# Layer 1 attention: the first bank of the next scores written before the values products, in two iterations

## The chip, the cores and the metric

The kernel runs on one core of a Trainium2 chip. The metric is the device time of one execution in microseconds (us), the median of several runs; less is better.

## The reference, cut to what matters

Two layers work on 512 latent tokens and 256 context tokens of width 1024. Layer 0 mixes by a bidirectional gated DeltaNet, layer 1 by attention with 8 query heads and 2 key heads of width 128. The change is in layer 1's attention alone:

```
def gqa_attend(q, k, v):
    b, lq, hq, d = q.shape
    qg = q.reshape(b, lq, ATT_KV_HEADS, hq // ATT_KV_HEADS, d)
    s = jnp.einsum('bqhgd,bkhd->bhgqk', qg, k).astype(F32) * (d ** -0.5)
    p = jax.nn.softmax(s, axis=-1).astype(v.dtype)
    return jnp.einsum('bhgqk,bkhd->bqhgd', p, v).reshape(b, lq, hq, d)
...
    y_lat = finish(blocked_gqa(ql, k_all, v_all), zl)      # finish: (o * silu(z)) @ w_out
...
return rms_norm(h_lat, final_norm_g)
```

Here `k_all` and `v_all` hold 768 tokens, context and latent ones together; the queries are the 512 latent ones.

## The kernel before

A float32 product is made of three products on TensorE: each operand is kept as a rounded high part and a low part, and `PASS` lists high by high, high by low and low by high.

Attention is one loop written out for `u` in 0 to 35 (`for u in range(32 + 4)`). Each of the first 32 values of `u` stands for one query head `hq = u // 4` and one tile `t = u % 4` of 128 queries. The work is pipelined over iterations. In iteration `u` TensorE issues, in this order:

1. `scores(u)` (line 2260): the 128 x 768 scores of query tile `u`, 6 products into `s3`;
2. `turn(u - 2)` (line 2288): six transposes of the shares of tile `u - 2`;
3. the iteration's extra piece: query or gate projections while there are any (`u` up to 23: lines 2189 and 2240), nothing in iterations 24 and 25, and `out_block(u - 26, 0, pg)` (line 2323), six products of the output projection, in iterations 26 to 32;
4. `values(u2, ...)` (line 2309): half of a pair's products of shares and values, 9 products into `po`. Iterations 24 and 25 make the two halves of pair 10.

Beside it VectorE takes the row maxima of `s3` (`maxima`, lines 2266 and 2268), ScalarE the exponentials with their sums (`powers`, line 2275, which reads the whole half of `s3` of its `u`), VectorE a reciprocal (line 2276), ScalarE the scaled shares (`shares`, line 2281). Transposes are copied out by `turned` (ScalarE, line 2295) and `turned_lo` (VectorE, line 2301). In even iterations `gated` (lines 2315, 2317, 2318) multiplies a finished pair of values by its gate, ahead of the maxima.

`s3` is one tile of PSUM, 128 x 2 x 768 float32, which is three banks of 512. Even `u` use elements 0 to 767 and odd `u` elements 768 to 1535. So each has one bank to itself, called its own bank (elements 0 to 511 or 1024 to 1535), and half of the middle bank, called shared. `scores` makes the three products of 512 columns on the own bank first and then the three of 256 columns on the shared one.

TensorE, VectorE and ScalarE run in the order in which the code is written (`manual_schedule`); the framework puts in the semaphores. GpSimd and the DMA queues are ordered by the framework's planner. GpSimd splits the output weights into `wo` during these iterations (lines 2455 and 2456). In iterations 24 and 25 the maxima are kept in `pg[0]`, in the others in the free half of `po`'s bank. After the loop TensorE makes the rest of the output projection (line 2471), and a short chain of VectorE and ScalarE instructions (lines 2477 to 2557) normalises and sends the last rows.

Of the kernel before, what the change touches and what calls it, by code (L numbers as in the profile page):

```python
# [86 lines left out]
def backbone(tc, a, out):  # L87
# [1137 lines left out]
    for k in range(KT):  # L1225
        for h in steps:
            wh, wl = halves_of[h]
            for i in range(2):
                first = not k
# [58 lines left out]
    c = []  # L1288
# [29 lines left out]
    for n, (i, nb) in enumerate(((0, 4), (0, 5), (1, 0), (1, 2), (1, 1), (1, 3), (1, 4), (1, 5))):  # L1318
# [3 lines left out]
        first, through = nb >= 4 or nb < 2, []  # L1322
# [93 lines left out]
    for pair in range(3):  # L1416
        first = None
# [5 lines left out]
    for t in range(NT):  # L1423
        due = T0 + (185, 80, 315, 190, 30, 335)[t]
        U = [Piece("DVE", 2.15, due, j_turn, t, d, after=[solved[t // 2]] + (joined if t < 5 else []), takes=["U" if t < 5 else "U5"] if d == 0 else (), lands=0.1) for d in range(2)]
        u = U[0].takes[0]
# [764 lines left out]
    def q_squares(p, t):  # L2191
        for h in range(2):
            jk = tmp.tile([P, P], F32, tag="jk", name=f"qj{p}{t}{h}")
            S.activation(jk, q_bank(p, t)[:, h * P:(h + 1) * P], AF.Square, accum_out=qTs["s", p][:, t, h:h + 1])

    def q_cosines(p, t):
        x = q_bank(p, t).rearrange("p (h d) -> p h d", h=2)
        o = tmp.tile([P, 2, P], F32, tag="qr", name=f"qr{p}{t}", bufs=2)
        V.tensor_tensor(o, x, bcast(cg[0][:, t], 1, 2), ALU.mult)
        return o  # L2200

    def q_sines(p, t, o):

        x = q_bank(p, t).rearrange("p (h d) -> p h d", h=2)
        V.tensor_tensor(x, x, bcast(sg[0][:, t], 1, 2), ALU.mult)
        o4 = o.rearrange("p h (s d) -> p h s d", s=2)
        V.tensor_tensor(o4, o4, raw(x, 64, [[128, 2], [-64, 2], [1, 64]]), ALU.add)
# [4 lines left out]
    def q_norm_steps(p, room_, t0, t1):  # L2212

        n = 2 * (t1 - t0)
        s_ = qTs["s", p].rearrange("p t h -> p (t h)")[:, 2 * t0:2 * t1]
        x, t = (room_[:, i * 16:i * 16 + n] for i in range(2))
        y = rsp.tile([P, 8], F32, tag="qy", name=f"qy{p}{t0}")[:, 0:n]
        steps = [
            lambda: V.tensor_scalar(x, s_, 1.0 / P, EPS, ALU.mult, ALU.add),
            lambda: V.tensor_scalar(y.bitcast(I32), x.bitcast(I32), -0.5, float(0x5F3759DF), ALU.mult, ALU.add),  # L2220
        ]
        for i in range(3):
            to = s_ if i == 2 else y
            steps += [
                lambda: V.scalar_tensor_tensor(t, x, -0.5, y, ALU.mult, ALU.mult),
                lambda: V.tensor_tensor(t, t, y, ALU.mult),
                lambda to=to: V.scalar_tensor_tensor(to, t, 1.5, y, ALU.add, ALU.mult),
            ]
        return steps
# [12 lines left out]
    def z_tanh(hq):  # L2242
        zts[hq] = at.tile([P, NLAT], F32, tag="zt", name=f"zt{hq}", bufs=4)
        S.activation(zts[hq], z_bank(hq), AF.Tanh, scale=0.5)
# [5 lines left out]
        z_tanh(hq)  # L2250
        z_rest(hq)

    def scores(u):
        hq, t = divmod(u, 4)
        g, b = hq // 4, u % 2
        own, shared = (slice(0, 512), slice(512, 768)) if b == 0 else (slice(256, 768), slice(0, 256))
        for c in (own, shared):
            for n_, (i, j) in enumerate(PASS):
                q = qTs[hq // 2][i][:, hq % 2, t * P:(t + 1) * P]
                T.matmul(s3[:, b, c], q, kT[j][:, g, c], start=n_ == 0, stop=n_ == 2)  # L2260

    def maxima(u):
        hq, t = divmod(u, 4)
        b = u % 2
        top = (pg[0] if u in (24, 25) else spare)[:, b:b + 1]
        V.tensor_reduce(top, s3[:, b], AX.X, ALU.max, negate=True)
        nm_ = at.tile([P, 1], F32, tag="nm", name=f"nm{u}")
        V.tensor_tensor(nm_, top, qTs["s", hq // 2][:, t, hq % 2:hq % 2 + 1], ALU.mult)
        return nm_
# [13 lines left out]
    def turn(u, ps):  # L2283

        pr, _ = prs.pop(u)
        for i3 in range(2):
            for j in range(3):
                T.transpose(ps[i3][:, j, :], pr[:, (i3 * 3 + j) * P:(i3 * 3 + j + 1) * P], ident)  # L2288

    def turned(u, ps):  # L2290
        t = u % 4
        if t % 2 == 0:
            pTs[u // 2] = [at.tile([P, NT, 256], F32R, tag=f"pT{i}", name=f"pT{u // 2}_{i}") for i in range(2)]
        for i3 in range(2):
            S.copy(pTs[u // 2][0][:, i3 * 3:i3 * 3 + 3, (t % 2) * P:(t % 2 + 1) * P], ps[i3][:, :3])
# [15 lines left out]
    def gated(u2):  # L2311
        hq, c0 = u2 // 2, (u2 % 2) * 256
        pTs.pop(u2)
        y32 = po[:, 0:256]
        V.scalar_tensor_tensor(y32, y32, 0.5, zts[hq][:, c0:c0 + 256], ALU.mult, ALU.mult)
        ys = [y[:, hq, c0:c0 + 256] for y in yT]
        S.copy(ys[0], y32)
        V.tensor_tensor(ys[1], y32, ys[0], ALU.subtract)
# [61 lines left out]
    for u in range(32 + 4):  # L2380
        piece = pieces1[u] if u < len(pieces1) else None
        last = (q_products, 0, 3) if u == 0 else pieces1[u - 1] if u <= len(pieces1) else None
        turning = 2 <= u < 34
        if u < 32:
            scores(u)
        if u >= 6 and u % 2 == 0:
            gated((u - 6) // 2)
        ps = [tr_tile(f"pt{u}_{i3}") for i3 in range(2)]
        o = None
        if last and last[0] is q_products:  # L2390
            q_squares(*last[1:])
            o = q_cosines(*last[1:])
        elif last and u % 2 == 0:
            z_tanh(last[1])
        if u == 0:
            norms = q_norm_steps(0, spare[:, 16:48], 3, 4)
        if turning:
            turn(u - 2, ps)
            turned(u - 2, ps)
        nm_ = maxima(u) if u < 32 else None  # L2400
        if o is not None:
            q_sines(*last[1:], o)
        if turning:
            turned_lo(u - 2, ps)
        if last and last[0] is z_products and u % 2 == 0:
            z_rest(last[1])
        if u < 32:
            powers(u, nm_)
        if u % 8 == 6 and u < 24:
            norms = q_norm_steps(u // 8 + 1, pg[0][:, 256:288], 0, 4)  # L2410
        if u % 8 in (6, 7) or u == 1:
            some(norms, 7 if u % 8 == 6 else 99)
        for half in range(2):
            if piece and piece[0] is q_products:
                q_products(*piece[1:], range(half * 4, half * 4 + 4))
            elif piece:
                k0 = 4 * (u % 2) + 2 * half
                z_products(piece[1], range(k0, k0 + 2))
            elif half == 0 and 26 <= u < 33:
                out_block(u - 26, 0, pg)  # L2420
            elif half == 0 and u >= 33:
                s_all = raw(s3, 0, [[1, 3 * 512]])
                acc1 = [s_all[:, nh * 512:(nh + 1) * 512] for nh in range(2)]
                for k in ((0, 1, 2), (3, 4, 5), ())[u - 33]:
                    out_block(k, 1, acc1)
                if u == 35:
                    out_block(7, 0, pg)
            if half == 1 and o is not None:
                q_turned(*last[1:], o)
            if u == 32 and half == 0:  # L2430
                aq_c.__exit__(None, None, None)
                f2_c = tc.tile_pool(name="fo", bufs=2, side="right", reuse_waits="tile")
                f2 = f2_c.__enter__()
                fg = f2.tile([P, D], F32, tag="fg", name="fg", bufs=1)
                gate1 = f2.tile([P, 1, D], F32, tag="gate1", name="gate1", bufs=1)
                ss = f2.tile([P, 4, 3], F32, tag="ss", name="ss", bufs=1)
                dma(gate1, gate_d[1])
                for t in range(3):
                    load_hs(t)
                dma(fg, a["final_norm_g"].unsqueeze(0).partition_broadcast(P).squeeze(1))  # L2440
                G.tensor_scalar(fg, fg, -(2.0 ** 0.5), None, ALU.mult)
            if half == 1 and u >= 4:
                u2, h_ = divmod(u - 4, 2)
                values(u2, range(3 * h_, 3 * h_ + 3))
        if u < 32:
            shares(u)
        if u == 23:
            gemm_c.__exit__(None, None, None)
            wo_c = tc.tile_pool(name="wo", bufs=2, side="left", reuse_waits="tile")
            wp = wo_c.__enter__()  # L2450
            wo = [wp.tile([P, KT, D], F32R, tag=f"wo{i}", name=f"wo{i}", bufs=1) for i in range(2)]
            for k in range(KT):
                w = wp.tile([P, D], F32, tag="w", name=f"wf{k}", bufs=3)
                dma(w, a["att_w_out"][0, k * P:(k + 1) * P, :])
                G.tensor_copy(wo[0][:, k], w)
                G.tensor_tensor(wo[1][:, k], w, wo[0][:, k], ALU.subtract)
# [146 lines left out]
```

## Time and profile before

| | us |
|---|---|
| median of 3 runs | 1144.64 |
| lowest and highest run | 1141.11, 1145.9 |
| the profiled execution, device time | 1139.69 |
| the profiled execution, span from first to last instruction | 1137.5 |
| TensorE busy | 1106.4 (97% of the span) |
| VectorE, ScalarE, GpSimd busy | 787.5, 746.9, 603.1 |

A line of the timeline gives the start of a run of like instructions, the time from its start to its end, engine, line, what is written from what, and the count; the bracket gives the idle time of the engine ahead of it and what ended it. PE is TensorE's products, PEld its weight loads, DVE VectorE, ACT ScalarE, POOL GpSimd. Products overlap in TensorE's pipeline, so that a run's end lies some 0.25 us behind the start of the next.

### The profile page before, as it was taken

To read this page: it belongs to the slowest core of one execution; us is meant where nothing else is said; L and a number is where in the kernel's file an instruction comes from. 1 tells how busy PE (TensorE), PEld (TensorE's weight loads), DVE (VectorE), ACT (ScalarE), POOL (GpSimd) and SP (SyncE) were. 2 spreads that over 40 slices of the span, in tenths; PEclk is the share of its full clock that TensorE was granted. 3 is DMA by queue.
4 is the path that set the end of the run, shared out by engine and by line. 5 is a ranking of instruction groups with operands and counts; after the bars stand their busy time and mean duration, and the time that the engine had idled before them with its cause. 6 is when DMAs were issued, how large, how long until landed. Compare 5 with 4: busy or idle time off the path is not lost. (4 is left out here: it accounts for less than half of the span.)

```text
span 1137.5 us, 27228 instructions
## 1 busy us (share of the span) xinstructions
PE 1106.4 (97%) x10511; PEld 903.7 (79%) x10511; DVE 787.5 (69%) x1628; ACT 746.9 (66%) x1990; POOL 603.1 (53%) x525
## 2 busy tenths in 40 slices
PE   5999999999999999999999999999999999999997
PEld 2677788888888888888666666788877889989886
DVE  4785666688889988774678788445555477667647
ACT  4453554477787888756689888875776356666731
POOL 0564111329999999960675598656744353130820
PEclk9999999999999999999999999999999999999999
DMA  9489753765738887665998994676854112101323
GB/s 366 180 305 324 253 159 118 228 174 171 219 129 245 280 233 222 182 229 164 280 279 249 276 257 116 207 213 183 247 148 139 37 58 73 38 19 57 111 75 93
DMA packets 117106, 208.69 MB, mean 183 GB/s; under 512 B 12113, under 2 KB 76786, under 8 KB 111730
## 3 DMA queue, kind: packets, MB, share of 16 engines
q1 hardware_dynamic: 97202, 195.71, 55.8%
q10 hardware_dynamic: 19776, 11.25, 3.3%
q8 instruction: 83, 1.36, 0.5%
q14 instruction: 45, 0.37, 0.1%
HBM read 166.16 MB, written 40.67 MB: 182 GB/s over the span
## 5 line engine op out<-in xcount | busy, mean ns | idle before, releaser
L1768 PE MATMUL po<-woh,y 128*128 128x512 f32 x384 | 129.3, 401 | 0.0
L1706 POOL TENSOR_TENSOR wol<-wo,woh 128x1024 fp32r<-128x1024 f32 x32 | 77.3, 2416 | 54.3 <-ACT woh L1699 51.1
L810 POOL TENSOR_TENSOR X<-X,tmp 128x62 f32<-128x62 f32 (+15 forms) x93 | 99.5, 1070 | 7.3
L1594 POOL TENSOR_TENSOR S<-S,glb 128x512 f32<-128x512 f32 x80 | 81.8, 1044 | 36.4 <-PE ks L1585 36.1
L809 POOL TENSOR_TENSOR tmp<-L,X 128x62 f32<-128x62 f32 (+15 forms) x93 | 91.0, 979 | 6.7
L929 PE MATMUL g_z<-uh,wh_z 128*128 128x512 f32 (+1 forms) x256 | 88.0, 344 | 0.0
L929 PE MATMUL g_v<-uh,wh_v 128*128 128x512 f32 (+1 forms) x256 | 87.9, 344 | 0.0
L944 DVE SCALAR_TENSOR_TENSOR acc_v<-g_v,cwv,acc_v 128x510 f32<-128x510 f32 (+3 forms) x128 | 77.7, 614 | 14.7 <-ACT acc_v L936 11.3
L929 PE MATMUL g_z<-ul,wh_z 128*128 128x512 f32 (+1 forms) x256 | 86.2, 337 | 0.5 <-issue 0.5
L929 PE MATMUL g_v<-ul,wh_v 128*128 128x512 f32 (+1 forms) x256 | 86.1, 336 | 0.0
L929 PE MATMUL g_v<-uh,wl_v 128*128 128x512 f32 (+1 forms) x256 | 86.1, 336 | 0.0
L929 PE MATMUL g_z<-uh,wl_z 128*128 128x512 f32 (+1 forms) x256 | 86.1, 336 | 0.0
L1768 PEld LDWEIGHTS po<-woh,y 128*128 128x128 f32 x384 | 72.3, 188 | 15.5 <-issue 0.3
L1768 PE MATMUL po<-wol,y 128*128 128x512 f32 x192 | 75.5, 393 | 0.0
L1734 DVE SCALAR_TENSOR_TENSOR pt<-pt,og,z 128x128 f32<-128x128 f32 x96 | 34.4, 358 | 33.3 <-PE pt L1725 31.0
L555 POOL TENSOR_TENSOR kt<-kt,kss 128x768 f32<-128x768 f32 x8 | 11.6, 1472 | 85.6 <-DVE kss L183 57.0
L1585 PE MATMUL ks<-S,ck 128*64 128x256 f32 x352 | 55.5, 392 | 0.9 <-ACT o L1591 0.9
L1662 DVE TENSOR_TENSOR S<-su,S 128x512 f32<-128x512 f32 x80 | 51.5, 686 | 5.1 <-PE su L1648 3.4
L1588 DVE SCALAR_TENSOR_TENSOR r<-ks,negV,cv 128x128 f32<-128x128 f32 x176 | 52.4, 344 | 3.6 <-DMA cv<-v_d 1.9
L1585 PE MATMUL ks<-S,cq 128*64 128x256 f32 x352 | 53.7, 379 | 0.0
L929 PEld LDWEIGHTS g_z<-ul,wh_z 128*128 128x128 f32 x256 | 48.6, 190 | 5.4 <-issue 0.7
L929 PEld LDWEIGHTS g_z<-uh,wh_z 128*128 128x128 f32 x256 | 48.5, 190 | 5.2
(469 smaller groups left out, 3341.5 us busy)
## 6 DMA issues: line engine op xcount, KB each, us to landing
aw<-in_ada_late SPq DMA_DIRECT2D x16, 1024.0 KB, 7.5
wo<-in_dn_w_out SPq DMA_DIRECT2D x32, 512.0 KB, 3.9
cv<-v_d SPq DMA_DIRECT2D x22, 512.0 KB, 9.6
aw<-in_ada_first SPq DMA_DIRECT2D x8, 1024.0 KB, 11.4
w_z<-in_dn_w_in SPq DMA_DIRECT2D x16, 512.0 KB, 6.2
w_v<-in_dn_w_in SPq DMA_DIRECT2D x16, 512.0 KB, 4.8
v_d<-vt ACTq DMA_DIRECT2D x16, 384.0 KB, 4.2
cT<-t_d SPq DMA_DIRECT2D x12, 512.0 KB, 9.1
```

The costliest lines, as they stand in the source:

```text
L555: G.tensor_tensor(kt, kt, bcast(r[:, h % 2 * NT:(h % 2 + 1) * NT], 2, P), ALU.mult)
L809: G.tensor_tensor(tv, bcast(L[:, :, j + 1:, j], 3, j + 1), bcast(X[:, :, j, 0:j + 1], 2, n), ALU.mult)
L810: G.tensor_tensor(X[:, :, j + 1:, 0:j + 1], X[:, :, j + 1:, 0:j + 1], tv, ALU.subtract)
L929: T.matmul(ps[:, :m], w[:, k], u[:, k, c0:c0 + m], start=k == 0 and n_ == 0, stop=k == KT - 1 and n_ == 2)
L944: V.scalar_tensor_tensor(acc[:, c0 + lo:c0 + hi], ps[:, lo + j - 2:hi + j - 2], cwv[:, j, ct:ct + 1], acc[:, c0 + lo:c0 + hi], ALU.mult, A ...
L1585: T.matmul(ks[r0:r0 + 64, w], kq[w][:, hh, r0:r0 + 64], St[hh][:, d], start=True, stop=True)
L1588: V.scalar_tensor_tensor(r[:, 2 * j + i], ks[:, 0, i], negV[:, visit, t, h:h + 1], v[:, h], ALU.mult, ALU.add)
L1594: G.tensor_tensor(St[hh], St[hh], bcast(g_, 3, P), ALU.mult)
L1662: V.tensor_tensor(St[hh], sj, St[hh], ALU.add)
L1706: G.tensor_tensor(wl, raws.pop(n), halves[n][0], ALU.subtract)
L1734: V.scalar_tensor_tensor(pj, pj, og, raw(z, off, [[st_, 2], [1, 64]]), ALU.mult, ALU.mult)
L1768: T.matmul(acc[nh], y[i][:, j, :], ww[k][:, nh * 512:(nh + 1) * 512], start=h == 0 and x == 0, stop=h == VH - 1 and x == 2)
```

## The change

`scores` gets a form that makes only the three own-bank products. In iterations 24 and 25 this form is called for the next `u` (25 and 26) after the transposes and ahead of the values products. When the loop comes to `scores(25)` and `scores(26)`, only the three shared products are left to be made, at the place where all six were. The number of products stays the same, and no other engine's instructions are moved.

```diff
-    def scores(u):
+    begun = set()
+
+    def scores(u, first=False):
         hq, t = divmod(u, 4)
         g, b = hq // 4, u % 2
         own, shared = (slice(0, 512), slice(512, 768)) if b == 0 else (slice(256, 768), slice(0, 256))
-        for c in (own, shared):
+        for c in (own,) if first else (shared,) if u in begun else (own, shared):
             for n_, (i, j) in enumerate(PASS):
                 q = qTs[hq // 2][i][:, hq % 2, t * P:(t + 1) * P]
                 T.matmul(s3[:, b, c], q, kT[j][:, g, c], start=n_ == 0, stop=n_ == 2)
...
+            if half == 0 and u in (24, 25):
+                scores(u + 1, first=True)
+                begun.add(u + 1)
             if half == 1 and u >= 4:
                 u2, h_ = divmod(u - 4, 2)
                 values(u2, range(3 * h_, 3 * h_ + 3))
```

## The prediction

> **What bounds the kernel now.** I read the page's busy shares first, then the chain that ended last, then the waits of TensorE around the change, and last the timeline of iterations 23 to 27.
>
> ```profile
> span 1137.5 us, 27228 instructions
> PE 1106.4 (97%) x10511; PEld 903.7 (79%) x10511; DVE 787.5 (69%) x1628; ACT 746.9 (66%) x1990; POOL 603.1 (53%) x525
> ```
>
> TensorE is the bound: 97% busy, no other engine above 69%. In the attention loop this holds for every iteration but the two that the change touches. TensorE's waits from 1050 to 1068 us are one row (what waited, for what, us, times, longest), and its work in single iterations (stretch, length, busy time and count, granted clock, DMA) shows the same:
>
> ```profile
> PE s L2260 <- ACT pr L2275: 1.4, 2, 0.8
> ...
> 1054.58:1058.31 3.73, 2.94 (x24) 1.00 0.00 0
> 1058.31:1061.99 3.68, 3.03 (x22) 1.00 0.49 140
> 1061.99:1129.30 67.31, 67.31 (x390) 1.00 0.34 101
> ```
>
> So 1.4 us in all is what TensorE loses here, in two waits; from the scores of iteration 26 to its last product, 67.31 us on, it has no gap. The timeline of TensorE through these iterations:
>
> ```profile
> 1053.52 1.22 PE L2309 MATMUL po<-pT,vv 128*128 128x256 f32 x9
> 1054.58 1.23 PE L2260 MATMUL s<-kT,qT 128*128 128x512 f32 x6
> 1055.64 0.82 PE L2288 MATMUL pt<-ident,pr 128*128 128x128 f32 x6
> 1056.21 1.30 PE L2309 MATMUL po<-pT,vv 128*128 128x256 f32 x9
> 1058.31 1.31 PE L2260 MATMUL s<-kT,qT 128*128 128x512 f32 x6 [0.79 <-ACT pr L2275]
> 1059.46 0.82 PE L2288 MATMUL pt<-ident,pr 128*128 128x128 f32 x6
> 1060.03 1.30 PE L2309 MATMUL po<-pT,vv 128*128 128x256 f32 x9
> 1061.99 1.32 PE L2260 MATMUL s<-kT,qT 128*128 128x512 f32 x6 [0.65 <-ACT pr L2275]
> 1063.15 0.81 PE L2288 MATMUL pt<-ident,pr 128*128 128x128 f32 x6
> 1063.73 1.64 PE L2323 MATMUL pg<-wo,yT 128*128 128x512 f32 x6
> 1065.20 1.25 PE L2309 MATMUL po<-pT,vv 128*128 128x256 f32 x9
> 1066.30 1.28 PE L2260 MATMUL s<-kT,qT 128*128 128x512 f32 x6
> ```
>
> The scores at 1054.58 are those of u = 24, at 1058.31 of 25, at 1061.99 of 26. Iterations 24 and 25 have no extra piece, so scores(25) comes up right behind nine values products and finds the exponential of u = 24 still running. In the chain that ended last the same stretch reads (start, length, piece):
>
> ```profile
> 1055.99 0.97 DVE pg L2266
> ...
> 1057.17 1.09 ACT pr L2275 x2
> 1058.26 0.04 issue
> 1058.31 1.31 PE s L2260 x6
> ...
> 1060.86 1.09 ACT pr L2275 x2
> ...
> 1061.99 1.32 PE s L2260 x6
> ```
>
> **The question that decides.** The exponential of u = 24 reads elements 0 to 767 of `s3`, two banks. The own products of u = 25 write elements 1024 to 1535, the third bank, last read by the exponential of u = 23, over since 1052.60. If only real use counted, the own products could have begun when the values products were issued, and only the three shared ones would have had to wait. The end of that exponential, the first product of scores(25) alone, then the products that start around 1059.1:
>
> ```profile
> 1052.41 0.19 ACT L2275 ACTIVATION_READ_ACCUMULATOR pr<-s,nm,sq 128x1 f32 x1
> ...
> 1058.31 0.50 PE L2260 MATMUL s<-kT,qT 128*128 128x512 f32 x1 [0.79 <-ACT pr L2275]
> ...
> L2260 PE MATMUL s<-kT,qT x2: 283/338/394, 1058.9 to 1059.1; 128*128 128x512 f32 x1, 128*128 128x256 f32 x1
> ```
>
> The 512-wide product is an own one, the 256-wide ones are shared. So it is the first own product that waits for the exponential, and the shared ones follow 0.8 us later without a wait. The framework seems to order writes and reads of `s3` by the tile and not by the bank. The built program of before speaks for it at one more place: the first product of the last output tile onto elements 1024 to 1535 of `s3` carries a wait for VectorE's reading of elements 512 to 1023, another bank, and nothing else stands behind that count. The other reading is that the wait belongs to the shared products and is only put on the first of the group of six; against it stands that at u = 0 the built program puts the waits of the shared products on the shared products.
>
> **The change part by part.** Products: none is added or removed, six are moved (three in each iteration), with their weight loads. VectorE, ScalarE, GpSimd and the DMA queues keep their instructions and order. What is behind the moved products on TensorE is the nine values products of pair 10's half, and from there all else.
>
> Steps from the rows, start to start: values 1.06 (1053.52 to 1054.58), transposes 0.57 (1055.64 to 1056.21), six output products 1.47 (1063.73 to 1065.20), a group of scores after a wait 1.15 (1058.31 to 1059.46), of which 0.79 own and 0.36 shared; without a wait 1.06 (1054.58 to 1055.64), so 0.70 own.
>
> With the wait as it stands on the own products (my forecast):
>
> 1. The transposes of iteration 24 end at 1056.46 (1055.64 + 0.82). The exponential of u = 24 is not moved, so own(25) starts at 1058.31, as scores(25) does now. TensorE idles 1.85 instead of 0.79, since the values products, which were issued at 1056.21 beside ScalarE's work, now stand behind the wait. That cover is what the move gives up.
> 2. own(25) 1058.31, values 1059.10, shared(25) 1060.16, transposes 1060.52. These were at 1059.46: 1.06 later, the length of the values products.
> 3. The maxima of u = 25 need both banks, so they come 1.06 later too, and the exponential with them: own(26) starts at 1061.99 + 1.06 = 1063.05. TensorE is done with the transposes at 1061.34 and idles 1.7 instead of 0.65.
> 4. own(26) 1063.05, values 1063.84, shared(26) 1064.90, transposes 1065.26, output products 1065.83. These were at 1063.73: 2.10 later.
> 5. A third wait appears. Pair 10's values now end at about 1065.14, and `gated` stands ahead of the maxima of u = 26 on VectorE. At u = 24 the same order shows its length:
>
> ```profile
> 1054.78 0.43 DVE L2315 SCALAR_TENSOR_TENSOR po<-po,zt 128x256 f32<-128x256 f32 x1 [1.29 <-PE po L2309]
> 1055.65 0.42 DVE L2318 TENSOR_TENSOR yT<-po,yT 128x256 fp32r<-128x256 f32 x1 [0.44 <-ACT yT L2317]
> 1055.99 0.96 DVE L2266 TENSOR_REDUCE pg<-s 128x1 f32<-128x768 f32 x1
> ...
> 1056.98 0.16 DVE L2268 TENSOR_TENSOR nm<-pg,sq 128x1 f32<-128x1 f32 x1
> ```
>
> From the values' end (1053.52 + 1.22 = 1054.74) to the next scores (1058.31) it takes 3.57, and 2.40 to the product that ends the maxima (1056.98 + 0.16). So scores(27) can't start before 1065.14 + 3.57 = 1068.71. TensorE by itself would come there at 1065.83 + 1.47 + 1.10 (1065.20 to 1066.30) = 1068.40, or 1068.64 with the values held to 1067.54 by the maxima kept in `po`'s bank. scores(27) now starts at 1066.30: 2.4 later.
> 6. From there each iteration keeps its own distances. The tightest is the even one, where the exponential of u = 28 ends 0.29 ahead of scores(29) (1074.21 + 0.19 against 1074.69), and both move together:
>
> ```profile
> 1074.21 0.19 ACT L2275 ACTIVATION_READ_ACCUMULATOR pr<-s,nm,sq 128x1 f32 x1
> ...
> 1074.69 1.21 PE L2260 MATMUL s<-kT,qT 128*128 128x512 f32 x6
> ```
>
> TensorE has no gap up to its last product (the 67.31 us above), so nothing gives the 2.4 back. GpSimd's last two low parts of the output weights end at 1083.7, 4 us ahead of the output products that use the seventh (1087.76): a later TensorE can't be held by them, and one earlier by 2 us could not either.
>
> ```profile
> 1078.95 4.76 POOL L2456 TENSOR_TENSOR wo<-wf,wo 128x1024 fp32r<-128x1024 f32 x2
> 1087.76 1.63 PE L2323 MATMUL pg<-wo,yT 128*128 128x512 f32 x6
> ```
>
> Sum: +2.4 us. The profiled execution took 1139.69, with 2.19 around its span of 1137.5, so it would be 1142.1. The median of the runs shown is 1144.64, 4.95 above that execution; on it the forecast is 1147.0. This is 0.2%, less than the 0.5% that a measurement of this kernel can tell from no change (the three runs shown lie 0.4% apart).
>
> **The rivals.**
>
> *The own products run free.* If the wait belongs to the shared products alone and moves with them, own(25) is issued at 1056.21, values at 1056.91, shared(25) at 1058.31 when the exponential is done, transposes at 1058.67, own(26) 1059.24, values 1059.94. The exponential of u = 25 ends 0.79 earlier, so shared(26) starts at 1061.20, transposes 1061.56, output products 1062.13 instead of 1063.73. The `gated` order holds scores(27) to 1061.24 + 3.57 = 1064.81 instead of 1066.30: 1.5 us gained, 1143.1 on the median. For it: the data allow it. Against it: the row at 1058.31. The Trainium skill's page "PSUM — Partial Sum Buffer", section "PSUM bank collisions raise a hardware error", would have it this way: engines working on different banks run clean, and the rule there is to guard by bank and quadrant and not wider. By that rule the own bank needs no wait and the time is 1143.1. The row of the own product does not agree: it waited 0.79 for a reader of the other two banks. I give this rival 0.17, the share that I leave to the reading in which the wait is merely put at the head of the group.
>
> *Slower by a stall that comes back.* To be slower by over 0.5%, 5.7 us, the delay of step 5 has to repeat in even iterations 26, 28 and 30: the 0.29 ahead of scores(29) has to turn into a wait of 1.1 each time. That needs the maxima of an even u to come 1.4 later after the values than now. The distances there are TensorE's own and VectorE's fixed order, both unchanged, so this gets 0.04; the time is 1144.64 + 2.4 + 3 x 1.1 = 1150.3.
>
> *Nothing moves.* If the own wait stood and later slack swallowed the delay, the time would stay at 1144.6. The stretch from 1061.99 to 1129.30 has busy time equal to its length, so there is no slack to swallow it: 0.03.
>
> **How the numbers follow.** The forecast, +2.4, has 0.73; a gain of 1.5 has 0.17; no change 0.03; slower by over 0.5% 0.04; 0.03 are left for a time over 0.5% lower, for which I see no mechanism but the spread of runs. Forecast, free products and no change all lie within 0.5%: 0.93. The range has to hold the bounds of the unknown wait, 1143.1 to 1147.0, and the spread of the runs shown, 3.5 below the median and 1.3 above it: 1140 to 1150.5.
>
> **What would show each step right or wrong.** Right: at line 2260 the first own product of u = 25 waits for ScalarE about 1.85 us and that of u = 26 about 1.7, the values products of these iterations start after it, the first output products start 2.1 later relative to scores(24), and a small wait shows up ahead of the values or scores of iteration 26 or 27. Wrong: own products directly behind the transposes with no wait, the wait on 256-wide products, and a TensorE total of waits below 1.4 us. The prediction fails on time if waits appear in iterations 28 to 31, or if the planner moves GpSimd's or the queues' instructions.

## The result and the profile after

The changed kernel takes 1143.97 us in the median of 22 runs (1142.0 to 1149.01), the kernel before 1142.57 us in 22 runs (1139.08 to 1145.9). The ratio is 1.0022, with a 95% interval of 1.0012 to 1.0031: slower by 2.5 us (0.0022 x 1142.57), with an interval of 1.4 to 3.5; the two medians lie 1.4 us apart. That is inside the 0.5% that the prediction set as its bound for no change, but with 22 runs of each it is not nothing. The profiled execution took 1142.0 us, where the prediction had 1142.1 for it; that this fits to 0.1 is partly luck (step 6 below).

The busy shares and the waits of TensorE from 1050 to 1140 us, of the kernel after (what waited, for what, us in all, times, longest):

```profile
span 1139.8 us, 27228 instructions
PE 1105.9 (97%) x10511; PEld 903.1 (79%) x10511; DVE 791.3 (69%) x1628; ACT 749.0 (66%) x1990; POOL 600.9 (53%) x525
...
PE s L2262 <- ACT pr L2277: 3.6, 2, 1.9
PE po L2311 <- DVE nm L2270: 0.3, 1, 0.3
```

The work is the same, the span is 2.3 us longer, and TensorE waits 3.9 us where it waited 1.4. The lines have moved by two: 2262 is the scores, 2277 the exponential, 2290 the transposes, 2311 the values, 2317 to 2320 `gated`, 2325 the output products. The timeline of TensorE, kernel after:

```profile
1054.23 1.23 PE L2262 MATMUL s<-kT,qT 128*128 128x512 f32 x6
1055.30 0.81 PE L2290 MATMUL pt<-ident,pr 128*128 128x128 f32 x6
1057.96 0.97 PE L2262 MATMUL s<-kT,qT 128*128 128x512 f32 x3 [1.85 <-ACT pr L2277]
1058.77 1.22 PE L2311 MATMUL po<-pT,vv 128*128 128x256 f32 x9
1059.83 0.52 PE L2262 MATMUL s<-kT,qT 128*128 128x256 f32 x3
1060.18 0.82 PE L2290 MATMUL pt<-ident,pr 128*128 128x128 f32 x6
1062.71 0.96 PE L2262 MATMUL s<-kT,qT 128*128 128x512 f32 x3 [1.71 <-ACT pr L2277]
1063.52 1.22 PE L2311 MATMUL po<-pT,vv 128*128 128x256 f32 x9
1064.57 0.52 PE L2262 MATMUL s<-kT,qT 128*128 128x256 f32 x3
1064.92 0.82 PE L2290 MATMUL pt<-ident,pr 128*128 128x128 f32 x6
1065.50 1.64 PE L2325 MATMUL pg<-wo,yT 128*128 128x512 f32 x6
1067.38 1.33 PE L2311 MATMUL po<-pT,vv 128*128 128x256 f32 x9 [0.25 <-DVE nm L2270]
1068.56 1.27 PE L2262 MATMUL s<-kT,qT 128*128 128x512 f32 x6
```

The six products of a scores group are now two rows of three. The 512-wide ones, on the bank that nobody is reading any more, wait 1.85 and 1.71 us for ScalarE. The nine values products stand behind them and no longer run during that wait. The 256-wide ones, on the bank that really is being read, follow without a wait. The stretch from scores(24) to scores(27) is 14.33 us long (1068.56 - 1054.23); it was 11.72. The same stretches as in the table of before, the last one cut once more at scores(27). The first row is the last stretch of the kernel before, from its scores(27) on; the others are the kernel after:

```profile
1066.30:1129.30 63.00, 63.00 (x365) 54.84 (x363) 37.93 (x90) 24.44 (x51) 17.64 (x9) 1.00 0.31 94
...
1054.23:1057.96 3.73, 1.88 (x14) 1.50 (x12) 3.05 (x7) 2.82 (x6) 3.73 (x4) 1.00 0.00 0
1057.96:1062.71 4.75, 3.04 (x21) 2.66 (x21) 2.50 (x7) 2.89 (x5) 4.75 (x3) 1.00 0.46 124
1062.71:1068.56 5.85, 5.59 (x37) 4.85 (x37) 3.14 (x8) 3.16 (x6) 4.03 (x5) 1.00 0.52 169
1068.56:1131.55 62.99, 62.99 (x365) 54.83 (x363) 37.94 (x90) 24.51 (x51) 16.41 (x8) 1.00 0.30 91
```

(Stretch, its length, busy time and count of TensorE's products and weight loads, of VectorE, ScalarE and GpSimd, then clock, DMA share, GB/s.) In the last row TensorE is busy for the whole 62.99 us, where it took 63.00 before: nothing there gives time back.

### The profile page after: what moved, and what is told of

The parts are those of the page before. It is cut to its first block, busy times and chain, and to the rows that moved or that the text cites. A ratio compares the mean times of both kernels' runs of the same rounds, so it can differ in the third digit from the quotient of the medians.

```text
span 1139.8 us, 27228 instructions
## 1 busy us (share of the span) xinstructions
PE 1105.9 (97%) x10511; PEld 903.1 (79%) x10511; DVE 791.3 (69%) x1628; ACT 749.0 (66%) x1990; POOL 600.9 (53%) x525
## 5 line engine op out<-in xcount | busy, mean ns | idle before, releaser
L809 POOL TENSOR_TENSOR tmp<-L,X 128x62 f32<-128x62 f32 (+15 forms) x93 | 87.9, 945 | 6.7
L929 PEld LDWEIGHTS g_v<-ul,wh_v 128*128 128x128 f32 x256 | 48.5, 190 | 5.5 <-issue 0.8
```

Source lines behind the costliest of these rows:

```text
L809: G.tensor_tensor(tv, bcast(L[:, :, j + 1:, j], 3, j + 1), bcast(X[:, :, j, 0:j + 1], 2, n), ALU.mult)
L929: T.matmul(ps[:, :m], w[:, k], u[:, k, c0:c0 + m], start=k == 0 and n_ == 0, stop=k == KT - 1 and n_ == 2)
```

## The experiments

My theory was the forecast's: the framework orders `s3` as one tile, so the own-bank products wait for the exponential of the predecessor, and moving them ahead of the values takes the cover away. The rivals: that the wait belongs to the shared products and the slowing has another cause; that the chip itself needs the wait; and that what is lost is one stall only, not a price for each move.

**e1_early_everywhere: make the move in seven iterations instead of two.**

```diff
-            if half == 0 and u in (24, 25):
+            if half == 0 and 24 <= u < 31:
```

> The move of the own products is made in iterations 24 to 30 instead of 24 and 25, so for u = 25 to 31. Theory (the framework orders s3 by tile, so each moved own product waits for the exponential of its predecessor and holds the values products behind it): every moved group waits; from own(u) to own(u + 1) an odd u takes about 4.7 us and an even u about 5.8, against 4.17 an iteration in the changed kernel, and the total is 5.5 us over the changed kernel, 8 over the one before (7 to 9, ratio about 1.007). Rival (the 2.5 us measured come from elsewhere, from drift or from another stage): the time stays within 1 us of the changed kernel's, ratio about 1.002.

Measured: 1149.34 us (6 runs) against 1142.13, ratio 1.0059 with 1.0037 to 1.0081, 7.2 us by the medians. In the traces it is 79.81 us from scores(24) to the start of the last group of products, against 71.75 before: 8.06 longer, and 8 was expected. Waits of TensorE from 1050 to 1140 us, and three of the moved groups in its timeline:

```profile
PE s L2262 <- ACT pr L2277: 8.3, 7, 1.9
...
1070.31 0.96 PE L2262 MATMUL s<-kT,qT 128*128 128x512 f32 x3 [1.36 <-ACT pr L2277]
1075.07 0.97 PE L2262 MATMUL s<-kT,qT 128*128 128x512 f32 x3 [0.30 <-ACT pr L2277]
1080.86 0.96 PE L2262 MATMUL s<-kT,qT 128*128 128x512 f32 x3 [1.37 <-ACT pr L2277]
```

Seven moves, seven waits. The distances of the moved groups alternate between 4.76 (1070.31 to 1075.07) and 5.79 us (1075.07 to 1080.86), close to the 4.7 and 5.8 that the theory of a price for each move gave. In the iterations with an output block that block covers part of the exponential, so the waits are shorter there. The price is not: two iterations take 10.55 us (1070.31 to 1080.86), where the kernel before takes 8.39 from its scores(27) to scores(29) (1066.30 to 1074.69), which is 1.08 for each move. A single stall is ruled out.

**e10_early_24_again, e5_early_24_only, e6_early_25_only: each move alone.** The first two are the same kernel.

```diff
-            if half == 0 and u in (24, 25):
+            if half == 0 and u == 24:     # e5 and e10
+            if half == 0 and u == 25:     # e6
```

> The move is made in iteration 24 alone. Theory: own(25) waits 1.85 us for ScalarE, all six of scores(26) wait for the exponential of u = 25, 1.06 us later than before; nothing is added in iteration 26, so that from scores(24) to scores(27) it takes 12.8 us (before 11.72, changed 14.33): +1.1.

> The move is made in iteration 25 alone. Theory: scores(25) waits 0.79 us as before, own(26) waits 1.7, pair 10's values end 2.7 us later than before, and gated holds the maxima of u = 26 and scores(27): from scores(24) to scores(27) 13.2 us, +1.5. With the move in iteration 24 alone that adds up to the +2.6 of both.

> The kernel of e5 executed again. In e5 TensorE's granted clock fell to half for some 3 us behind the wait of 1.85 us, which e6 and the changed kernel did not show in their traces. Theory (the fall is not fixed to the code, it comes in some executions behind a wait of about 2 us): without it, scores(24) to scores(27) takes 12.8 us; with it, again 14.3. Either outcome gives the price of the move in iteration 24 alone: +1.1 without a fall of the clock.

Measured, one execution each: e5 1148.37 and e6 1144.56 us, beside a run of before of 1141.89; e10 1144.5 us. The distance from scores(24) to scores(27) says more than one time can: 14.27 us in e5, 12.76 in e10, 13.24 in e6, against 11.72 before. Timelines of TensorE, first e10, then e6, then e5:

```profile
1062.07 0.95 PE L2262 MATMUL s<-kT,qT 128*128 128x512 f32 x3 [1.85 <-ACT pr L2277]
1062.86 1.22 PE L2311 MATMUL po<-pT,vv 128*128 128x256 f32 x9
...
1066.80 1.33 PE L2262 MATMUL s<-kT,qT 128*128 128x512 f32 x6 [0.66 <-ACT pr L2277]
```

```profile
1065.34 0.96 PE L2262 MATMUL s<-kT,qT 128*128 128x512 f32 x3 [1.71 <-ACT pr L2277]
...
1070.01 1.32 PE L2311 MATMUL po<-pT,vv 128*128 128x256 f32 x9 [0.25 <-DVE nm L2270]
```

```profile
1064.46 1.30 PE L2262 MATMUL s<-kT,qT 128*128 128x512 f32 x3 [1.85 <-ACT pr L2277]
1065.55 2.13 PE L2311 MATMUL po<-pT,vv 128*128 128x256 f32 x9
```

The move at 24 costs 12.76 - 11.72 = 1.04 us, the length of the values products (1.06); the scores of 26, not moved here, still wait their 0.66. The move at 25 costs 13.24 - 11.72 = 1.52: the values products again (1.05), and the values of iteration 26, which start 0.42 later behind the output products than before (1.89 for 1.47; the third wait, 0.25 of idle time) and take 0.06 longer. Together 2.56, against 2.61 with both moves. In e5 the same nine values products take 2.13 us where e10 has 1.22: behind the wait the clock was lower, which cost 14.27 - 12.76 = 1.5 us more in that execution. That is a matter of the clock, told at the end; the forecast had no term for it.

In e6 the own products of 26 wait 1.71 us alone, with no shared product beside them. This rules out the reading that the wait is only put at the head of a group.

**e2_split_tiles and e3_split_tiles_early: one tile for each bank, without the move and with it.** `s3` becomes `sA`, `sM` (middle bank) and `sB`; maxima and exponentials are made in two pieces each. The product that ended the maxima joins theirs; the two sums of the exponentials are joined by one more instruction.

```diff
-    s3 = pS.tile([P, 2, NTOK], F32, tag="s3", name="s3")
+    sA, sM, sB = (pS.tile([P, 512], F32, tag=f"s{x}", name=f"s{x}") for x in "AMB")
+    parts = [[(sA, slice(0, 512)), (sM[:, 0:256], slice(512, 768))], [(sB, slice(256, 768)), (sM[:, 256:512], slice(0, 256))]]
...
+        for x, (s_, c_) in enumerate(parts[u % 2]):
+            S.activation(pr[:, c_], s_, AF.Exp, ..., accum_out=sm[:, x:x + 1])
+        V.tensor_tensor(sm[:, 0:1], sm[:, 0:1], sm[:, 1:2], ALU.add)
```

> The order of the kernel before, but the three banks of s3 are three tiles; maxima and exponentials are made in two pieces each and their results joined. Theory: the 512-wide own products of u = 25 and 26 no longer wait for ScalarE and follow the values products directly; the wait appears on the 256-wide shared ones. Longer maxima (0.1 to 0.2 us) and exponentials (0.4) eat part of it; scores(27) comes 0.6 us earlier than in the kernel before, total -0.6 us (-1.2 to +1). Rival (the own bank itself is not free until the exponential of the predecessor is done): the 512-wide products still wait, and the longer exponential makes the kernel 1 us slower or more.

> The three tiles of the run before, with the changed order: own(25) and own(26) ahead of the values products. Theory: with the wait off the own products the move is free, since own and values products together fit ahead of the end of the exponential in either order; scores(24) to scores(27) within 0.2 us of the three tiles in the old order, no wait on 512-wide products, time the same within 0.3 us, where the same move costs 2.6 us with one tile. Rival (the move itself costs, by the values products' place): 1 to 2.5 us slower than the three tiles in the old order.

Measured: e2 1154.01 us, ratio 1.0111 (1.0085 to 1.0136); e3 1153.42 us, ratio 1.01 (1.0074 to 1.0127), 6 runs each against 1142.13. Timelines around scores(25), TensorE and one row of ScalarE in e2, then TensorE in e3:

```profile
1060.19 1.31 PE L2313 MATMUL po<-pT,vv 128*128 128x256 f32 x9
1061.34 0.86 PE L2260 MATMUL sB<-kT,qT 128*128 128x512 f32 x3
1062.95 0.62 PE L2260 MATMUL sM<-kT,qT 128*128 128x256 f32 x3 [0.76 <-ACT pr L2277]
...
1061.48 0.78 ACT L2277 ACTIVATE pr<-sA,nm,sq 128x512 f32<-128x512 f32 x1 [0.48 <-DVE nm L2269]
```

```profile
1060.63 0.94 PE L2262 MATMUL sB<-kT,qT 128*128 128x512 f32 x3
1061.41 1.21 PE L2315 MATMUL po<-pT,vv 128*128 128x256 f32 x9
1063.40 0.62 PE L2262 MATMUL sM<-kT,qT 128*128 128x256 f32 x3 [0.77 <-ACT pr L2279]
```

These lines decide the question of the prediction. With a tile for each bank the own products run without a wait, directly behind the values (e2) or ahead of them (e3), and the wait has gone to the 256-wide products. In e2 they write `sB` from 1061.34 to 1062.20 while ScalarE reads `sA` from 1061.48 on. In e3 they are done at 1061.57, before that exponential starts at 1061.93, so e3 alone would not show that the two can run at once. The move then costs nothing: scores(24) to scores(27) is 14.03 us in e2 and 14.08 in e3 (their times lie 0.6 apart where I had expected 0.3, with 7 us between the runs of each). So the chip did not need the wait on the own bank; the tile that spans three banks made it. Whether it needs the one on the middle bank, whose two halves are different elements, no run tested. The Trainium skill's page "PSUM — Partial Sum Buffer", section "PSUM bank collisions raise a hardware error", has engines on different banks running clean, and its rule is to guard by bank and quadrant, or simply by bank, and not by address. By that rule, e2 agrees. That a guard must not be wider, as the prediction put it, is an inference and not the page's sentence.

But both are 11 to 12 us slower than before, where I had expected a small gain from e2. The added sum was slow in places; e2's VectorE, then its GpSimd:

```profile
1066.49 1.35 DVE L2278 TENSOR_TENSOR sm<-sm 128x1 f32<-128x1 f32 x1 [0.68 <-ACT pr L2277]
...
1072.86 2.25 DVE L2278 TENSOR_TENSOR sm<-sm 128x1 f32<-128x1 f32 x1 [0.55 <-ACT pr L2277]
...
1060.76 7.06 POOL L2460 TENSOR_TENSOR wo<-wf,wo 128x1024 fp32r<-128x1024 f32 x3
...
1072.70 4.71 POOL L2460 TENSOR_TENSOR wo<-wf,wo 128x1024 fp32r<-128x1024 f32 x2
```

The new sum of two columns of 128 numbers takes 1.35 and 2.25 us where GpSimd is in the middle of its subtractions, and the next maxima and values products stand behind it.

**e8_split_one_input and e9_split_one_input_early: the same pair, with the two sums joined by an instruction that reads one tensor and a scalar.**

```diff
-        V.tensor_tensor(sm[:, 0:1], sm[:, 0:1], sm[:, 1:2], ALU.add)
+        V.tensor_scalar(sm[:, 0:1], sm[:, 0:1], sm[:, 1:2], None, ALU.add)
```

> The three tiles of e2 with one change: the two partial sums are joined by an instruction with one tensor input and a scalar operand instead of two tensor inputs in SBUF. Theory (in e2 that sum, at 1.35 and 2.25 us for one column, stood behind GpSimd, and with it gated, the maxima and the values products): it takes 0.2 us, the waits of the values products for the maxima (5.6 us in e2) fall below 0.5, and the kernel is within 1.5 us of the one before, -1 at best. Rival (the two-piece maxima and exponentials make the chain too long by themselves): waits of 3 us or more stay and it is 4 us or more slower.

> The kernel of e8 with own(25) and own(26) ahead of the values products. Theory: as in e3 against e2 the move is free once the own bank is a tile of its own: scores(24) to scores(27) within 0.1 us of e8, times within 0.5 us. Rival: the move costs 1 us or more here too.

Measured: e8 1146.96 us (10 runs), ratio 1.0042 (1.0027 to 1.0057); e9 1146.22 (12 runs), ratio 1.0038 (1.0019 to 1.0056); before 1142.76. The line's 32 instructions in e8 (shortest, median, longest in ns), and a row of TensorE's waits in e8:

```profile
L2278 DVE TENSOR_SCALAR sm<-sm x32: 204/213/217, 928.9 to 1094.4; 128x1 f32<-128x1 f32 x32
...
PE po L2313 <- DVE nm L2269: 1.6, 3, 1.1
```

No instruction of this kind is over 217 ns now, and the distance to before falls from 11.9 us (1154.01 - 1142.13) to 4.2 (1146.96 - 1142.76). Scores(24) to scores(27) is 12.90 us in e8 and 12.83 in e9: with a tile for each bank the move is free a second time. That the 4.2 stay I had not expected. At u = 24 the two-piece maxima take 1.48 us for 1.15 before, the exponentials 1.42 for 1.08, and the values products into `po` wait 1.6 us in all for maxima. From scores(24) to the start of the last group the trace has 73.92, against 71.75 before. That names only a part of the 4.2; the rest stays open.

**e4_fill_with_output, e7_fill_psum, e11_fill_both, e12_fill_25_only: leave the order, put other work into the waits.** Output products are made one iteration earlier, so that some of them lie in iterations 24 and 25, where nothing covered the exponential. The maxima of 24 and 25 can then not be kept in the bank that the output products write: e4 puts them in SBUF, e7 and e11 elsewhere in PSUM, and e12, which fills 25 alone, moves those of 25 only. e7 overwrites a column of `pg[1]` that is still to be read, which spoils that column, so it is no kernel to use; e11 and e12 keep the maxima of u = 24 out of `pg[1]`. The number of output products in iterations 24 to 32:

```diff
-            elif half == 0 and 26 <= u < 33:
-                out_block(u - 26, 0, pg)          # 0 0 6 6 6 6 6 6 6
+                out_ahead(...)                    # e4:      2 4 6 6 6 6 6 6 0
+                                                  # e7, e11: 2 3 6 5 6 5 6 6 3
+                                                  # e12:     0 3 6 5 6 5 6 6 5
```

> The order of scores and values is that of the kernel before. The empty places in iterations 24 and 25 are filled with the first six products of the output projection: two that need only the high part of the weights in 24, four in 25; iterations 26 to 31 make the next six each, iteration 32 none; the maxima of u = 24 and 25 go to SBUF. Theory (the two iterations lose 1.4 us because TensorE has too little work there until the exponential is done): TensorE's waits for ScalarE shrink to about 0.3 us in all, iteration 32 falls away, total -1.4 us against before (-1.6 to -0.8), ratio about 0.9988. Rival (the gaps are bound by the chain over maxima and exponentials, and the output products will wait for GpSimd's split of the weights when they come earlier): waits for POOL of 1 us or more appear at the output products, total 0.

> The filling with output products once more, without the two faults that e4 showed. The maxima of u = 24 and 25 stay in PSUM (in pg[1]), so that their product with the row scale has one input in SBUF and not two; and the output products are dealt out as 2, 3, 6, 5, 6, 5, 6, 6, 3 over iterations 24 to 32 instead of leaving iteration 32 empty. Theory (TensorE lacks work in 24 and 25, and VectorE's small product was held up by GpSimd in e4): the product of line 2268 takes 0.16 us again, TensorE's waits for ScalarE fall from 1.4 to 0.5 us or less, no wait at the values of iteration 32, total -1.2 us against before (-1.5 to -0.6), ratio 0.999. Rival (another bound takes over, as in e4): waits of 1 us or more in all stay, total 0 or slower.

> e7 wrote the maxima of u = 24 into a column of pg[1] that the gate of head 7 was still to be read from, and so spoilt that column; here the maxima of u = 24 go to the usual place in po's bank and those of u = 25 to pg[1], when it is free. All else as in e7. Theory: the values products of iteration 24 now wait for the maxima of u = 24, which costs up to 0.2 us; TensorE's waits in 24 and 25 are 0.7 us or less in all, total -1.1 us against before (-1.4 to -0.5), ratio 0.999. Rival: the maxima in po's bank hold up the exponential of u = 24 by more than the filling gains, total 0.

> Only iteration 25 is filled (three output products), iteration 24 is left as it was, with its maxima in pg[0]; dealt out as 0, 3, 6, 5, 6, 5, 6, 6, 5. Theory: the wait of 0.79 us at scores(25) stays, the one of 0.65 at scores(26) goes, total -0.6 us against before. It is the half of e11 that leaves the maxima of u = 24 alone. Rival: nothing gained, 0.

Measured, 12 runs each: e4 1144.8 us beside 1142.13 of before, ratio 1.0031 (1.0012 to 1.0049), slower. e7 1140.43 us beside 1142.76, 0.999 (0.9975 to 1.0006); e11 1139.38 and e12 1139.92 us beside 1140.86, 0.9997 (0.9979 to 1.0015) and 0.9996 (0.9981 to 1.0011). None of these three can be told from before. In e4 VectorE and TensorE show why:

```profile
1058.34 2.19 DVE L2268 TENSOR_TENSOR nm<-tp,sq 128x1 f32<-128x1 f32 x1
...
1061.70 1.32 PE L2260 MATMUL s<-kT,qT 128*128 128x512 f32 x6 [2.35 <-ACT pr L2275]
1062.86 1.45 PE L2288 MATMUL pt<-ident,pr 128*128 128x128 f32 x6
```

With the maxima in SBUF, the product of two columns that took 0.16 us takes 2.19, beside GpSimd again; the exponential comes late, the wait grows from 0.79 to 2.35, and the transposes behind it take 1.45 for 0.82, at a lower clock. A second loss is in iteration 32, left without output products: there the values wait 0.73 for `gated`. With the maxima in PSUM (e11) the waits ahead of the scores are gone:

```profile
1057.26 0.71 PE L2327 MATMUL pg<-wo,yT 128*128 128x512 f32 x2
1058.44 1.32 PE L2309 MATMUL po<-pT,vv 128*128 128x256 f32 x9 [0.46 <-DVE nm L2268]
1059.59 1.28 PE L2260 MATMUL s<-kT,qT 128*128 128x512 f32 x6
```

Only the 0.46 is left, where the values wait for the maxima that now lie in `po`'s bank. From scores(24) to the start of the last group of products it is 71.10 us in e11, 71.06 in e7 and 71.05 in e12, against 71.75 before and 74.35 after. So covering the wait is worth some 0.7 us in the trace, and the times cannot tell that from nothing. None of these kernels is shown to beat the kernel before.

## Why the prediction was right, step by step

- **Step 1** held: the own products of 25 waited 1.85 us, as forecast, and started 3.73 us after scores(24), as scores(25) did before. The move gave up the cover and gained nothing.
- **Step 2** held: the transposes come 5.95 us after scores(24) (1060.18 - 1054.23), before 4.88, so 1.07 later for 1.06.
- **Step 3** held: 1.71 us of wait at 26 for a forecast of 1.7.
- **Step 4** held: the output products come 11.27 us after scores(24), before 9.15, so 2.12 later for 2.10.
- **Step 5** had the right chain, `gated` ahead of the maxima, but was 0.2 short and took the wrong one of two waits: scores(27) came 2.61 later, not 2.41. The sum took its 1068.71 from scores(27) waiting for the exponential, and had 1068.64 by the values waiting for the maxima. In the run the values wait 0.25 and scores(27) does not wait. For their start I took the chain of u = 24, 2.40 us from the values' end to the last of the maxima. There the maxima went to `pg[0]`, and the reduction started 0.34 us after the start of `gated`'s last instruction, while that was still running. At u = 26 they go to the bank that `gated` reads. The chain that ended last, kernel after (start, length, piece), and the same two instructions at u = 26 in the kernel before:

```profile
1065.64 0.44 DVE yT L2320
...
1066.17 0.98 DVE po L2268
...
1067.17 0.17 DVE nm L2270
1067.38 1.33 PE po L2311 x9
```

```profile
1063.39 0.42 DVE L2318 TENSOR_TENSOR yT<-po,yT 128x256 fp32r<-128x256 f32 x1 [0.93 <-ACT yT L2317]
1063.92 0.97 DVE L2266 TENSOR_REDUCE po<-s 128x1 f32<-128x768 f32 x1
```

  The reduction starts 0.53 after the start of that instruction, behind its end, so the stretch is 2.60 (1064.74 to 1067.34). The kernel before has the same 0.53 at u = 26, so the profile that I had would have given it; and in e11, where the maxima of u = 24 go to `po`'s bank, it is 0.53 at u = 24 too (1056.69 to 1057.22). It goes with the bank and not with the iteration. The values start 0.19 later than the 1067.54 that the prediction named, once the 0.35 is counted by which this execution is ahead at scores(24), and they take 1.18 to the next scores instead of 1.10. With the 0.07 between the two waits that is the 0.2 (0.19 + 0.08 - 0.07).
- **Step 6** held: TensorE is busy all of the 62.99 us behind. The execution was 0.35 ahead at scores(24), and -0.35 + 2.61 = 2.26 is the span's 2.3. The 0.35 and the 0.2 that step 5 was short nearly cancel, which is why 1142.1 fits the profiled execution so well.

**The rivals.** *Own products run free* fell for this kernel: its sign was a wait on 256-wide products. That sign showed in e2 and e3, so the rival was right about the chip and wrong about the tile. *The stall that comes back* did not show: no wait in iterations 28 to 31. *Nothing moves* fell with the third wait and the full last stretch.

**The level and the range.** The difference was right: +2.4 forecast, 2.61 in the trace, 2.5 by the ratio with 1.4 to 3.5, though only 1.4 by the medians. But 1147.0 us was 3 too high. Of that 2.1 came from its base, the median of three runs, 1144.64, where twenty-two put the kernel before at 1142.57, and 1.0 from the medians lying closer than the forecast. Three runs 5 us apart do not give a level to within 2 us. The range does not follow from its terms either: 1143.1 - 3.5 and 1147.0 + 1.3 give 1139.6 to 1148.3, not 1140 to 1150.5. The measured median lies in both.

## What to carry to other kernels

Look at which instruction of a group carries the wait, and how wide it is, before moving part of the group: a wait that comes from a tile's bounds moves with the part that did not need it. Moving work from behind its cover to ahead of it, while what it waits for stays, costs the length of the cover, at each place where it is done. Split the tile by what is really shared first, and count what the split adds on the other engines: here it made the move free and cost more than the move could bring.

## What the runs showed of the hardware

A one-column instruction of VectorE with both inputs in SBUF is not always short. Beside GpSimd's subtraction (one is 2.4 us) the sum of two columns took 1.35 and 2.25 us in e2, and the product of two columns 2.19 in e4; with a scalar in place of the second tensor none of the 32 was over 0.217, and with one input in PSUM the product took 0.16 before, beside a subtraction too (1056.98, in one that runs from 1056.79). The slow ones ended when the subtraction that was running did: the first at 1067.84, where GpSimd's row ends at 1067.82, and the other two within 0.05 us of it, an estimate that divides GpSimd's rows evenly among their subtractions. The Trainium skill's page "SBUF — State Buffer", section "Who interferes with whom", says that an instruction of VectorE with two SBUF inputs contends with one of GpSimd that reads SBUF, and that one with a single SBUF input, outside the 2-port modes, does not. By that rule, these rows agree.

TensorE's clock fell behind a wait of under 2 us in one execution and not in another. The stretches behind the own products' wait of 1.85 us, in e5 and then in e10, the same kernel:

```profile
1064.45:1070.01 5.56, 5.55 (x30) 5.19 (x30) 2.06 (x6) 2.20 (x4) 5.56 (x4) 0.69 0.50 142
```

```profile
1062.07:1066.80 4.73, 4.07 (x31) 3.74 (x31) 2.50 (x7) 2.88 (x5) 4.73 (x3) 1.00 0.53 125
```

The granted clock was 0.69 in the mean in the one and 1.00 in the other, for 1.5 us of time. It was 0.50 behind the 2.35 in e4 as well (1063.96 to 1065.81), and in e3 behind a wait of 2.19 (1073.07 to 1074.35), but 1.00 in e2 behind one of 2.24 (1071.43 to 1074.35). The Trainium skill's page "TensorE: Matmul & The Clock Gate", section "Why this matters for your kernels", tells to keep gaps under some 3 us, and its Part 1 says that the window is free-running. In the runs here the clock fell behind gaps of 1.85, 2.19 and 2.35 us, which are under that figure; that the fall differs between executions of one kernel is what a free-running window would give, but no run tested that. Whether it is why the runs after reach further up (1149.01) than those before (1145.9) is not shown: the run of 1149.01 has a mean clock of 0.994, one of 1142.31 has 0.993, and among the runs of the kernel before beside e1 one took 1147.65.
